# A four-layer decoder step on one core: cache transfers placed between weight tiles, and weight splits placed ahead of a triangular solution

## The chip, the cores and the metric

The kernel runs on one core of a Trainium2 chip. The metric is the device time of one execution in microseconds (us). The core has five engines with an instruction queue each: TensorE (PE, matrix products; its weight loads are listed as PEld), VectorE (DVE), ScalarE (ACT), GpSimd (POOL) and SyncE (SP). An engine works through its queue in order: an instruction that waits holds up all that stand behind it. Nearly all DMA transfers are issued from SP's queue (SPq in the rows) and carried out by 16 DMA engines.

## The reference

One step of a trunk of four layers, for a prompt of 256 tokens and 8 samples of 4 tokens, 288 columns in all, 1024 wide, in float32. Layer i mixes tokens by sliding-window attention (i mod 3 = 0: layers 0 and 3), a gated delta rule (layer 1) or a gated linear recurrence (layer 2). A feed-forward part stands before and behind each mixer.

```
for i in range(4):
    x = x + 0.5 * swiglu(rms(x), w_in[i, 0], w_out[i, 0])    # 1024 -> 2 x 2816 -> 1024
    x = x + mixer_i(rms(x))
    x = x + 0.5 * swiglu(rms(x), w_in[i, 1], w_out[i, 1])

# attention, sample group: the caches hold the last 128 keys and values
kk = concat([cache_k, k]);  vv = concat([cache_v, v])        # 128 + 4 rows
o  = softmax_with_sink(mask(q kk^T)) vv
new_cache_k, new_cache_v = kk[:, 4:], vv[:, 4:]              # outputs

# delta rule, prompt group, chunks of 64, 16 value heads
a   = strict_lower((k*beta) k^T) * decay
sol = triangular_solve(1 + a, [v*beta, k*beta*exp(gcum)])
```

So 124 of the 128 rows of every new cache are old rows, copied from the input to the output.

## The kernel before

**The weight stream.** Weights come from DRAM once and are the bulk of the traffic. The class Stream holds two lists: chunks (a raw tile of 128 x 4 x 256 float32, 512 KB, one DMA at L51) and jobs (half a chunk each in the feed-forward stages). Four raw tiles exist (RAW = 4). A job is split first: ACT writes the rounded part hi (L67), then DVE the rest lo = raw - hi (L68). PE then runs twelve matmuls into one accumulator: for each of four slices of 128 rows hi times the high part of the activations (L93), hi times their low part (L94), and lo times their high part (L95). Up to two jobs are split ahead of the one that PE works on (AHEAD = 2, three buffers each for hi and lo). When both jobs of a raw tile are split, the load of the next tile into its buffer is written down, and SP issues it once the buffer is free. The evacuations of the accumulators and all mixer work stand between the jobs.

**Order.** The code is recorded, and a scheduler then fixes each engine's order from what depends on what and from the place in the code. `tc.high_priority(n)` moves what is recorded in it to an earlier place, by n steps; PRIO is 5000. `tc.issue_after(ins)` keeps what is recorded in it behind the instruction `ins` on that instruction's engine. Within what these allow, an engine's order is fixed when the program is built.

**Attention caches** (layers 0 and 3). load_values loads all cached values into one tile vc (L402, 1 MB) and stores rows 4 to 127 of it to the output (L403). cache_unit, called four times with two samples each, does the same for the keys (kc, L407 and L408, 256 KB each) and transposes them. The scheduler moves these transfers forward as far as their buffers are free: SP issues several of them in the feed-forward stage ahead of the attention.

**Delta net** (layer 1, 800 to 1194 us). Its jobs come in the order gates, k, q, half of z, v, the other half of z. When the last k is there, DVE forms the triangular blocks and solve_unit inverts 32 x 32 diagonal blocks, 128 at a time: they go through DRAM into a layout with one block per partition (L953 to L956), DVE does 31 elimination steps of products (L965) and subtractions (L968) on the tile X, a copy transposes it (L969), and the result goes back through DRAM (L970 to L978). merge_unit then joins the 32-blocks to 64-blocks on PE (L989, L993). All of this is recorded at high priority, PRIO. sample_inverse_unit does the small inverse of the samples (matmuls L931, L933, L936 on tiles iv). Then the eight heads follow: conv on each v, v_unit (L1033 transposes the values), core_unit (the chunks of the prompt) and sample_unit with the samples' states (loaded at L1044). conv is L676 to L686.

Of the kernel before, what the change touches and what calls it, by code (L numbers as in the profile page):

```python
# [11 lines left out]
AF = mybir.ActivationFunctionType  # L12
ALU = mybir.AluOpType
# [2 lines left out]
T = 288  # L16
D = 1024
DFF = 2816
EPS = 1e-6
RAW, AHEAD, NT = 4, 2, 6  # L20
CW = 256
# [2 lines left out]
class Stream:  # L24

    def __init__(self, nc, raw, split, psum):
        self.nc, self.raw, self.split_pool, self.psum = nc, raw, split, psum
        self.chunks, self.jobs = [], []  # L30
        self.loaded, self.tiles, self.left = 0, {}, {}
        self.nsplit, self.parts = 0, {}
        self.njob = 0
        self.accs = {}
        self.pooled = set()
        self.held, self.mms, self.tags = [], [], {}

    def chunk(self, loads):
        self.chunks.append(loads)
# [6 lines left out]
    def load(self, upto):  # L46
        while self.loaded < min(upto, len(self.chunks)):
            c = self.loaded
            t = self.raw.tile([128, 4, CW], F32, tag="raw", name="raw", bufs=RAW)
            for sl, src in self.chunks[c]:  # L50
                self.nc.sync.dma_start(out=sl(t), in_=src)  # L51
            self.tiles[c] = t
            self.loaded += 1

    def split_to(self, upto):
        while self.nsplit < min(upto, len(self.jobs)):
            j = self.nsplit
            chunk, view, nk, m = *self.jobs[j][:3], self.jobs[j][8]
            self.load(chunk + 1)
            src = view(self.tiles[chunk])  # L60
            hi = self.split_pool.tile([128, 4, 128], F32R, tag="hi", name="hi", bufs=AHEAD + 1)
            lo = self.split_pool.tile([128, 4, 128], F32R, tag="lo", name="lo", bufs=AHEAD + 1)
            h, l = hi[:, :nk, :m], lo[:, :nk, :m]
            if len(src.shape) == 4:
                h = h.rearrange("p k (a b) -> p k a b", a=src.shape[2])
                l = l.rearrange("p k (a b) -> p k a b", a=src.shape[2])
            self.nc.scalar.activation(out=h, in_=src, func=AF.Copy)  # L67
            (self.nc.gpsimd if j in self.pooled else self.nc.vector).tensor_tensor(out=l, in0=src, in1=h, op=ALU.subtract)  # L68
            self.parts[j] = hi, lo
            self.nsplit += 1  # L70
            self.left[chunk] -= 1
            if not self.left[chunk]:
                self.tiles.pop(chunk)
                self.load(chunk + 1 + RAW)
# [28 lines left out]
PRIO = 5000  # L103
# [4 lines left out]
def trunk(ctx: ExitStack, tc: tile.TileContext, I, consts, O):  # L108
    nc = tc.nc
# [12 lines left out]
        def tile(shape, dt, tag, name):  # L122
            return psum.tile(shape, dt, tag=tag, name=name, bufs=PSUM_BUFS[tag])

    st = Stream(nc, raw, split, Acc)

    def misc(tag="ma"):
        return Acc.tile([128, 512], F32, tag, tag)
# [12 lines left out]
    class Slabs:  # L141


        def __init__(self, dt):
            self.dt, self.t = dt, {}
# [43 lines left out]
    def w_in_group(w, c0, key, evacs, m=128):  # L189

        for a in range(0, len(evacs), 2):
            n, c1, cs = len(evacs[a:a + 2]), c0 + a * m, []
            for kc in range(2):
                src = w[kc * 512:(kc + 1) * 512, c1:c1 + n * m].rearrange("(k p) c -> p k c", p=128)
                cs.append(st.chunk([((lambda t, n=n: t[:, :, :n * m]), src)]))
            if key not in begun:
                st.tags.update({(key, c1, e): "c%d" % e for e in range(n)} if TG else {})
            cells = [(kc, e) for kc in range(2) for e in range(n)]
            for kc, e in cells if key not in begun else sorted(cells, key=lambda c: c[1]):
                st.job(cs[kc], col(e, m), 4, xs_of(key, range(kc * 4, kc * 4 + 4)), (key, c1, e),  # L200
                       kc == 0, kc == 1, evacs[a + e], m=m)
            begun.add(key)
# [191 lines left out]
    def swa(i, j):  # L394
        key = ("m", i)
        w = I["swa_w_in"][j]
        L = {}

        def load_values():
            L["vc"] = mx(2048, "vc", 1).rearrange("p (b f) -> p b f", b=8)  # L400
            L["kT8"] = mx(2048, "kT8", 1).rearrange("p (g b j) -> p g b j", g=2, b=8)
            nc.sync.dma_start(out=L["vc"], in_=I["cache_swa_v"][j].rearrange("b j g d -> j b (g d)"))  # L402
            nc.sync.dma_start(out=O[8][j, :, 0:124].rearrange("b j g d -> j b (g d)"), in_=L["vc"][4:128])  # L403

        def cache_unit(b):
            kc = mx(512, "kc", 2).rearrange("p (b f) -> p b f", b=2)
            nc.sync.dma_start(out=kc, in_=I["cache_swa_k"][j, b:b + 2].rearrange("b j g d -> j b (g d)"))  # L407
            nc.sync.dma_start(out=O[7][j, b:b + 2, 0:124].rearrange("b j g d -> j b (g d)"), in_=kc[4:128])  # L408
            ps = misc()
            for a in range(2):  # L410
                for gp in range(2):
                    PE.transpose(ps[:, (gp * 2 + a) * 128:(gp * 2 + a + 1) * 128],
                                 kc[:, a, gp * 128:(gp + 1) * 128], ident)
            S.activation(out=L["kT8"][:, :, b:b + 2, :], in_=ps.rearrange("p (g b j) -> p g b j", g=2, b=2),
                         func=AF.Copy)
# [19 lines left out]
        def ev_kv(ps, m):  # L435
            if m == 0:
                L["kv"] = half()
                L["m4"] = mx(1024, "m4", 1)
                L["vtok"] = L["m4"][:, 0:512].rearrange("p (c f) -> p c f", c=2)
                L["ktok"] = L["m4"][:, 512:768]  # L440
                tables()
            if m < 2:
                rope(L["kv"][:, m], ps, "")
            else:
                V.tensor_tensor(out=L["kv"][:, m], in0=ps[:, :T], in1=nrm[key]["rbc"], op=ALU.mult)
            if m == 3:
                kv_tok_unit()
# [129 lines left out]
        def q_jobs(m0):  # L577
            for kc in range(2):
# [6 lines left out]
                for e in range(2):  # L585
                    st.job(c, (lambda t, e=e: t.rearrange("p k (a h d) -> p k a h d", a=2, h=2)[:, :, :, e]), 4,
                           xs_of(key, range(kc * 4, kc * 4 + 4)), (key, "q", m0 + e), kc == 0, kc == 1,
                           lambda ps, m=m0 + e: ev_q(ps, m))

        w_in_group(w, 1024, key, [lambda ps, m=m: ev_kv(ps, m) for m in range(4)])  # L590
        for m0 in (0, 2, 4):
            q_jobs(m0)
# [15 lines left out]
    def gdn(i, j):  # L608
        key = ("m", i)
        w = I["gdn_w_in"][j]  # L610
        L = {"st": {}, "vs": {}, "vt": {}, "u": {}}
# [628 lines left out]
        def run():  # L1240
            with tc.tile_pool(name="early", bufs=1, reuse_waits="tile") as M[1]:
                history()
                norm_run(key, False)
                st.run(34 + 8 * ZE - NJ)
                sample_inverse_unit()
            NW[0] = 7
            with tc.tile_pool(name="late", bufs=1, reuse_waits="tile") as M[1]:
                st.run(16)
                cores(0, 4)
                st.run(16)  # L1250
                cores(4, 8)
                st.run(32 - 8 * ZE)
                for kh in range(KS // 2):
                    gate(kh)
                st.run(2 * KS)
                for kh in range(KS // 2, 8):
                    gate(kh)
                st.run(32 - 2 * KS)
# [479 lines left out]
```

## Time and profile before

| | us |
|---|---|
| median of 3 runs | 2683.88 |
| lowest, highest | 2674.12, 2688.52 |
| the profiled execution: time | 2682.05 |
| the profiled execution: span | 2680.2 |
| PE busy in the span | 2575.3 (96%) |
| DVE busy in the span | 1763.5 (66%) |
| mean granted clock of PE | 0.976 of full speed |

The span runs from the first to the last instruction that the profiler saw; the profiled execution's time is 1.85 us more. PE's matmuls overlap, so a matmul's listed length (0.30 us) is longer than the distance at which the next one starts. The granted clock (PEclk) is 1.00 at 2.4 GHz and 0.50 at 1.2 GHz; it is 1.00 for most of the program. A high busy share of PE says that little can be won by moving work; what can be won shows in the short stretches in which PE waits, and in those at clock 0.50 that follow them.

### The profile page before, as it was taken

How to read it: one execution, taken by the hardware profiler on the slowest of the kernel's cores; microseconds unless marked ns; L12 is line 12 of the kernel's file. 1: busy time of each engine (PE TensorE's matmuls, PEld its weight loads, DVE VectorE, ACT ScalarE, POOL GpSimd, SP SyncE). 2: the span in 40 equal slices, each digit the busy share in tenths (PEclk: the TensorE clock that was granted, in tenths of full speed). 3: DMA queues.
4: the chain of work that ended last, by engine and by line, in shares of the span. 5: the costliest groups of instructions: out<-in, count | busy, mean ns of one | idle time of the engine just before them, and what ended most of it. 6: DMA issues, size and time to landing. Idle time of an engine off the chain costs nothing.

```text
span 2680.2 us, 52736 instructions
## 1 busy us (share of the span) xinstructions
PE 2575.3 (96%) x20268; PEld 2430.8 (91%) x20268; DVE 1763.5 (66%) x3772; ACT 1413.6 (53%) x3129; POOL 250.3 (9%) x404
## 2 busy tenths in 40 slices
PE   7999999999999799999999999888999999999998
PEld 6999799999997677689999999676899999979998
DVE  5666776666567756667666656877666665667655
ACT  4555555455455356665555544666455554465543
POOL 1000100000002134430000000443000000010000
PEclk9999999999999898899999999999999999999999
DMA  6555345555553354455555555344555555533553
GB/s 191 166 160 168 82 133 166 165 163 168 162 161 105 93 145 123 123 155 164 162 165 163 168 166 162 98 129 130 178 160 165 165 166 165 172 94 111 171 163 124
DMA packets 442370, 400.14 MB, mean 149 GB/s; under 512 B 24491, under 2 KB 439973, under 8 KB 442117
## 3 DMA queue, kind: packets, MB, share of 16 engines
q1 hardware_dynamic: 441492, 395.66, 49.0%
q8 instruction: 159, 2.61, 0.4%
q10 hardware_dynamic: 624, 1.11, 0.1%
q14 instruction: 95, 0.77, 0.1%
HBM read 374.64 MB, written 22.07 MB: 148 GB/s over the span
## 4 chain that ended last, share of the span: by engine, by line
PE 76%; issue 11%; DVE 6%; DMA 2%; POOL 2%; ACT 2%; SPq 0%; DVEq 0%; POOLq 0%; ACTq 0%
PE acc L93 22%; PE acc L95 22%; PE acc L94 22%; DVE lo L68 1%; DMA raw<-in_ffn_w_in_dram 1%; DMA kc<-in_cache_swa_k_dram 1%; PE c L513 1%; PE c L1163 1%; PE s L528 1%; PE c L1454 0%; PE ma L520 0%; DVE acc L682 0%; ACT hi L67 0%; PE c L1168 0%; DVE W L1380 0%
## 5 line engine op out<-in xcount | busy, mean ns | idle before, releaser
L93 PE MATMUL acc<-sl,hi 128*128 128x288 f32 x5384 | 1617.1, 301 | 21.6 <-ACT hi L67 13.4
L95 PE MATMUL acc<-sl,lo 128*128 128x288 f32 x5384 | 1607.8, 299 | 19.1 <-DVE lo L68 18.9
L94 PE MATMUL acc<-sl,hi 128*128 128x288 f32 x5384 | 1612.2, 299 | 1.8 <-DVE sl L1487 1.8
L67 ACT ACTIVATE hi<-raw 128x512 fp32r<-128x512 f32 (+1 forms) x1378 | 853.2, 621 | 992.6 <-PE acc L94 920.8
L68 DVE TENSOR_TENSOR lo<-raw,hi 128x512 fp32r<-128x512 f32 (+1 forms) x1378 | 952.6, 693 | 592.6 <-ACT hi L67 537.3
L95 PEld LDWEIGHTS acc<-sl,lo 128*128 128x128 f32 x5384 | 1025.9, 191 | 32.9 <-DVE lo L68 21.9
L93 PEld LDWEIGHTS acc<-sl,hi 128*128 128x128 f32 x5384 | 1021.8, 190 | 34.7 <-ACT hi L67 16.1
L94 PEld LDWEIGHTS acc<-sl,hi 128*128 128x128 f32 x5384 | 1023.4, 190 | 14.0 <-issue 10.1
L272 POOL TENSOR_TENSOR r<-v,roots 128x3 f32<-128x3 f32 x5 | 5.8, 1162 | 1867.3 <-DVE v L292 1867.3
L362 DVE TENSOR_TENSOR sil<-acc,sil 128x288 f32<-128x288 f32 x176 | 79.8, 457 | 54.3 <-PE acc L95 50.9
L355 DVE TENSOR_TENSOR sil<-acc,rbc 128x288 f32<-128x288 f32 x176 | 79.7, 457 | 50.5 <-PE acc L95 50.2
L364 DVE TENSOR_TENSOR sl<-sil,sl 128x288 fp32r<-128x288 f32 x176 | 78.9, 452 | 0.0
L356 ACT ACTIVATE sil<-sil 128x288 f32<-128x288 f32 x176 | 77.6, 445 | 2.0 <-DVE sil L355 1.9
L363 ACT ACTIVATE sl<-sil 128x288 fp32r<-128x288 f32 x176 | 77.5, 444 | 0.6 <-DVE sil L362 0.6
L242 ACT ACTIVATE sl<-x,gT 128x288 fp32r<-128x288 f32 x96 | 51.0, 536 | 26.0 <-DVE x L379 15.4
L682 DVE SCALAR_TENSOR_TENSOR acc<-buf,cw,acc 128x312 f32<-128x312 f32 x96 | 57.8, 606 | 4.2 <-ACT acc L680 2.0
L245 DVE SCALAR_TENSOR_TENSOR sl<-x,gT,sl 128x288 fp32r<-128x288 f32 x96 | 50.6, 532 | 0.2
L498 ACT ACTIVATE e<-e,m 128x128 f32<-128x128 f32 (+1 forms) x72 | 32.6, 454 | 17.0 <-DVE m L495 16.8
L258 ACT ACTIVATE sq<-x 128x288 f32<-128x288 f32 x91 | 38.7, 431 | 5.1 <-DVE x L379 5.1
L255 DVE TENSOR_TENSOR ssq<-ssq,sq 128x288 f32<-128x288 f32 x84 | 37.9, 451 | 0.1
L1113 POOL TENSOR_TENSOR st<-st,ex 128x512 f32<-128x512 f32 x32 | 35.7, 1136 | 17.4 <-PE ma L1080 17.4
L495 DVE CUSTOM_DVE_ANT_0 e<-c,sl,sink 128x128 f32<-128x128 f32 (+1 forms) x72 | 27.8, 419 | 13.4 <-PE c L513 10.6
(435 smaller groups left out, 1847.8 us busy)
## 6 DMA issues: line engine op xcount, KB each, us to landing
raw<-in_ffn_w_in_dram SPq DMA_DIRECT2D x352, 512.0 KB
raw<-in_ffn_w_out_dram SPq DMA_DIRECT2D x128, 512.0 KB
raw<-in_ffn_w_out_dram SPq DMA_DIRECT2D x64, 384.0 KB
raw<-in_gdn_w_in_dram SPq DMA_DIRECT2D x48, 512.0 KB
raw<-in_hgrn_w_in_dram SPq DMA_DIRECT2D x32, 512.0 KB
out_dram<-st SPq DMA_DIRECT2D x24, 512.0 KB
raw<-in_swa_w_in_dram SPq DMA_DIRECT2D x32, 256.0 KB
raw<-in_swa_w_out_dram SPq DMA_DIRECT2D x32, 256.0 KB
```

What stands on the lines that cost most here:

```text
L67: self.nc.scalar.activation(out=h, in_=src, func=AF.Copy)
L68: (self.nc.gpsimd if j in self.pooled else self.nc.vector).tensor_tensor(out=l, in0=src, in1=h, op=ALU.subtract)
L93: mm(ps, hi[:, i, :m], xh(), start=start and i == 0, stop=False)
L94: mm(ps, hi[:, i, :m], xl(), start=False, stop=False)
L95: self.mms.append(mm(ps, lo[:, i, :m], xh(), start=False, stop=stop and i == last).ins)
L242: S.activation(out=h[m], in_=x[:, m], func=AF.Identity, scale=g)
L355: V.tensor_tensor(out=t, in0=ps[:, :T], in1=nrm[key]["rbc"], op=ALU.mult)
L356: S.activation(out=t, in_=t, func=AF.Silu)
L362: V.tensor_tensor(out=t, in0=ps[:, :T], in1=t, op=ALU.mult)
L363: S.activation(out=h, in_=t, func=AF.Copy)
L364: V.tensor_tensor(out=l, in0=t, in1=h, op=ALU.subtract)
L682: V.scalar_tensor_tensor(out=a[:, 0:312], in0=b[:, t:t + 312], scalar=cw[:, 32 * t + mt:32 * t + mt + 1], in1=a[:, 0:312], op0=ALU.mult, o ...
```

## The change

Two things, independent of each other.

1. **Cache transfers of the attention layers.** Stream notes the DMA of each raw tile (loads). load_values and cache_unit wrap their DMAs in issue_after, so that each stands on SP behind a given raw tile of the feed-forward stage ahead of the attention: the load of vc behind tile 16, its store behind tile 24, the key loads behind tiles 28, 36, 44 and 52, and their stores six tiles later. L["before"] counts where that stage begins (FFN_CHUNKS is its number of tiles: 22 x 2 for w_in and 24 for w_out). Each store of 124 rows becomes two, of 112 and of 12 rows.
2. **Splits in the delta net's first part.** While the jobs up to the second z group are recorded, with the sample inverse, Stream.first is 2 * PRIO: the splits (L67, L68 before; L71, L72 now) are recorded at that priority, ahead of the solution at PRIO. Elsewhere first is 0.

```diff
@@ Stream @@
+        self.loads = {}
+        self.first = 0
...
-                self.nc.sync.dma_start(out=sl(t), in_=src)
+                self.loads[c] = self.nc.sync.dma_start(out=sl(t), in_=src).ins
...
-            self.nc.scalar.activation(out=h, in_=src, func=AF.Copy)
-            (self.nc.gpsimd if j in self.pooled else self.nc.vector).tensor_tensor(out=l, in0=src, in1=h, op=ALU.subtract)
+            with self.tc.high_priority(self.first):
+                self.nc.scalar.activation(out=h, in_=src, func=AF.Copy)
+                (self.nc.gpsimd if j in self.pooled else self.nc.vector).tensor_tensor(out=l, in0=src, in1=h, op=ALU.subtract)
@@ swa @@
+        def behind(n):
+            return tc.issue_after(st.loads[L["before"] + n])
+
+        def store(dst, src):
+            for a, n in ((0, 112), (112, 12)):
+                nc.sync.dma_start(out=dst[:, a:a + n].rearrange("b j g d -> j b (g d)"), in_=src[4 + a:4 + a + n])
...
-            nc.sync.dma_start(out=L["vc"], in_=I["cache_swa_v"][j].rearrange("b j g d -> j b (g d)"))
-            nc.sync.dma_start(out=O[8][j, :, 0:124].rearrange("b j g d -> j b (g d)"), in_=L["vc"][4:128])
+            with behind(16):
+                nc.sync.dma_start(out=L["vc"], in_=I["cache_swa_v"][j].rearrange("b j g d -> j b (g d)"))
+            with behind(24):
+                store(O[8][j], L["vc"])
...
-            nc.sync.dma_start(out=kc, in_=I["cache_swa_k"][j, b:b + 2].rearrange("b j g d -> j b (g d)"))
-            nc.sync.dma_start(out=O[7][j, b:b + 2, 0:124].rearrange("b j g d -> j b (g d)"), in_=kc[4:128])
+            with behind(28 + 4 * b):
+                nc.sync.dma_start(out=kc, in_=I["cache_swa_k"][j, b:b + 2].rearrange("b j g d -> j b (g d)"))
+            with behind(34 + 4 * b):
+                store(O[7][j, b:b + 2], kc)
...
+        L["before"] = len(st.chunks) - FFN_CHUNKS
@@ gdn, run @@
+                st.first = 2 * PRIO
                 st.run(34 + 8 * ZE - NJ)
                 sample_inverse_unit()
+                st.first = 0
```

The orders of the engines stand as follows. SP's queue in the first feed-forward stage, before, from the load of the cached values on (x3 means three in a row):

```order
L402 DMA vc<-in_cache_swa_v_dram 128x8x256
L51 DMA raw<-in_ffn_w_in_dram 128x4x256 x3
L403 DMA out_dram<-vc 124x8x256
L407 DMA kc<-in_cache_swa_k_dram 128x2x256
L51 DMA raw<-in_ffn_w_in_dram 128x4x256
L407 DMA kc<-in_cache_swa_k_dram 128x2x256
L408 DMA out_dram<-kc 124x2x256
```

The same place now, with twelve further raw tiles ahead of the first cache transfer:

```order
L54 DMA raw<-in_ffn_w_in_dram 128x4x256 x12
L416 DMA vc<-in_cache_swa_v_dram 128x8x256
L54 DMA raw<-in_ffn_w_in_dram 128x4x256 x8
L410 DMA out_dram<-vc 112x8x256
L54 DMA raw<-in_ffn_w_in_dram 128x4x256
L410 DMA out_dram<-vc 12x8x256
L54 DMA raw<-in_ffn_w_in_dram 128x4x256 x3
L423 DMA kc<-in_cache_swa_k_dram 128x2x256
L54 DMA raw<-in_ffn_w_in_dram 128x4x256 x6
L410 DMA out_dram<-kc 112x2x256
```

The cache transfers have moved from the stage's start to places between its raw tiles, at least one tile apart.

DVE's queue in the middle of the solution, before, around the elimination step with blocks of 12 and 13 columns:

```order
L968 TENSOR_TENSOR X<-X,tmp 128x10x12 x2
L965 TENSOR_TENSOR tmp<-A,X 128x130
L965 TENSOR_TENSOR tmp<-A,X 128x117
L968 TENSOR_TENSOR X<-X,tmp 128x10x13
L968 TENSOR_TENSOR X<-X,tmp 128x9x13
```

The same steps now:

```order
L983 TENSOR_TENSOR tmp<-A,X 128x120
L72 TENSOR_TENSOR lo<-raw,hi 128x512
L983 TENSOR_TENSOR tmp<-A,X 128x120
L986 TENSOR_TENSOR X<-X,tmp 128x10x12 x2
L983 TENSOR_TENSOR tmp<-A,X 128x130
L983 TENSOR_TENSOR tmp<-A,X 128x117
L72 TENSOR_TENSOR lo<-raw,hi 128x512
L986 TENSOR_TENSOR X<-X,tmp 128x10x13
L986 TENSOR_TENSOR X<-X,tmp 128x9x13
```

Lo parts of the weight stream (L72) now stand between the products and subtractions of the solution.

PE's queue at the end of the merge and the sample inverse, before (L993 is the merge, L1149 the first head):

```order
L95 MATMUL acc<-sl,lo 128x288
L931 MATMUL s<-iv 32x32 x16
L993 MATMUL c_10992<-sl,tmp 32x32
L933 MATMUL s<-iv 32x32 x16
L936 MATMUL s<-iv,cst 128x512
L993 MATMUL c_10992<-sl,tmp 32x32 x31
L1149 MATMUL c_12291<-cst,sl 64x128 x8
```

The sample inverse's last two products now (L951 and L954, which were L933 and L936):

```order
L99 MATMUL acc<-sl,lo 128x288
L951 MATMUL s<-iv 32x32 x16
L97 MATMUL acc<-sl,hi 128x288
L98 MATMUL acc<-sl,hi 128x288
L99 MATMUL acc<-sl,lo 128x288
L97 MATMUL acc<-sl,hi 128x288
L98 MATMUL acc<-sl,hi 128x288
L99 MATMUL acc<-sl,lo 128x288
L954 MATMUL s<-iv,cst 128x512
```

The sample inverse, which stood inside the merge, now stands ahead of it among stream matmuls. The merge's first matmul (L989 before, L1007 now) has 5725 stream matmuls ahead of it before and 5865 now, counted from the program's start; between the merge's last matmul and the first transposes of values (L1033, now L1051) stood 139 and stand 33.

## Rows read from the trace of the kernel before

**Rows 1.** The page: its span, and each engine's busy us, share and instructions.

```profile
span 2680.2 us, 52736 instructions
...
PE 2575.3 (96%) x20268; PEld 2430.8 (91%) x20268; DVE 1763.5 (66%) x3772; ACT 1413.6 (53%) x3129; POOL 250.3 (9%) x404
```

**Rows 2.** Stretches: us, busy PE, PEld, DVE, ACT, POOL; PEclk, DMA share, GB/s.

```profile
20.00:24.00 4.00, 4.00 (x31) 3.89 (x30) 3.93 (x9) 1.49 (x4) 1.64 (x2) 1.00 1.00 333
32.00:38.00 6.00, 5.60 (x42) 5.36 (x42) 4.62 (x10) 4.72 (x10) 0.00 (x0) 1.00 0.26 87
49.20:52.40 3.20, 3.20 (x12) 2.82 (x12) 0.94 (x2) 0.18 (x1) 0.00 (x0) 0.50 0.52 156
...
100.00:110.00 10.00, 10.00 (x77) 10.00 (x76) 6.52 (x12) 5.04 (x10) 0.00 (x0) 1.00 0.48 152
```

**Rows 3.** Waits, 40 to 60 us: who waited for whom, us, times, longest.

```profile
ACT hi L67 <- DMA raw<-in_ffn_w_in_dram: 14.1, 2, 8.4
...
PE acc L93 <- ACT hi L67: 8.4, 2, 5.2
```

**Rows 4.** Timeline of SP's queue, 5 to 110 us: start, us, instruction.

```profile
16.77 0.42 SPq L402 DMA_DIRECT2D vc<-in_cache_swa_v_dram  x1
21.08 6.65 SPq L51 DMA_DIRECT2D raw<-in_ffn_w_in_dram  x3
27.82 0.41 SPq L403 DMA_DIRECT2D out_dram<-vc  x1
```

**Rows 5.** Timeline of SP and ACT, 121.5 to 131 us.

```profile
121.66 8.37 SPq L51 DMA_DIRECT2D raw<-in_ffn_w_in_dram  x4
...
129.87 0.63 ACT L67 ACTIVATE hi<-raw 128x512 fp32r<-128x512 f32 x1 [0.96 <-PE acc L94]
```

**Rows 6.** Stretches of the feed-forward stage ahead of the last layer.

```profile
1890.00:1896.00 6.00, 6.00 (x47) 6.00 (x46) 5.41 (x13) 4.97 (x10) 0.00 (x0) 1.00 0.27 94
1916.90:1919.90 3.00, 2.94 (x12) 2.94 (x13) 2.86 (x9) 0.69 (x2) 0.00 (x0) 0.50 0.05 18
```

**Rows 7.** Waits of PE, 1895 to 1925 us.

```profile
PE acc L93 <- ACT hi L67: 5.0, 2, 2.7
```

**Rows 8.** Stretches in the delta net.

```profile
887.30:903.20 15.90, 0.02 (x2) 0.02 (x1) 15.86 (x84) 0.00 (x0) 0.00 (x0) 0.50 0.00 1
903.20:906.30 3.10, 3.10 (x13) 3.10 (x14) 3.10 (x18) 0.50 (x1) 0.00 (x0) 0.51 0.08 5
800.00:940.00 140.00, 117.03 (x1231) 99.01 (x1230) 102.40 (x337) 63.22 (x154) 27.53 (x79) 0.91 0.36 100
```

**Rows 9.** Timeline of PE; in brackets the idle time before and its releaser.

```profile
903.18 0.61 PE L95 MATMUL acc<-sl,lo 128*128 128x288 f32 x1 [15.88 <-DVE lo L68]
```

**Rows 10.** DVE by line, 882 to 915.3 us: busy us, mean ns, idle before.

```profile
L682 DVE SCALAR_TENSOR_TENSOR acc<-buf,cw,acc 128x312 f32<-128x312 f32 x10 | 5.4, 537 | 0.0
L68 DVE TENSOR_TENSOR lo<-raw,hi 128x512 fp32r<-128x512 f32 x7 | 4.8, 680 | 0.0
```

**Rows 11.** Line L965: ns min/median/max, first and last start, forms.

```profile
L965 DVE TENSOR_TENSOR tmp<-A,X x60: 163/242/281, 882.3 to 913.2; 128x110 f32<-128x110 f32 x5, 128x120 f32<-128x120 f32 x5, 128x126 f32<-128x126 f32 x5, 128x56 f32<-128x56 f32 x4
```

**Rows 12.** Timeline of SP's queue, 820 to 1000 us.

```profile
914.54 0.41 SPq L970 DMA_DIRECT2D XD<-X  x1
...
919.94 1.00 SPq L974 DMA_DIRECT2D xc<-XD  x2
...
947.45 4.09 SPq L1044 DMA_DIRECT2D st<-in_state_gdn_dram  x4
```

**Rows 13.** Lines L989 and L1033 on PE: ns min/median/max, first and last start.

```profile
L989 PE MATMUL c<-xc,sl x128: 190/191/213, 926.2 to 934.1; 32*32 32x32 f32 x128
...
L1033 PE MATMUL ma<-cst,v x32: 270/272/331, 971.4 to 1145.0; 128*128 128x128 f32 x32
```

**Rows 14.** PE by line, 926 to 971 us: busy us, mean ns, idle before.

```profile
L936 PE MATMUL s<-iv,cst 32*128 32x512 f32 x2 | 1.9, 1062 | 0.7 <-ACT iv L934 0.7
...
L933 PE MATMUL s<-iv 32*32 32x32 f32 x32 | 1.2, 192 | 0.8 <-DVE iv L932 0.8
```

More of the change, by code (lines that the diff above doesn't have):

```diff
@@ L18 @@
 DFF = 2816
+FFN_CHUNKS = DFF // 128 * 2 + 24
 EPS = 1e-6
@@ L24, with __init__ @@
 class Stream:
-    def __init__(self, nc, raw, split, psum):
-        self.nc, self.raw, self.split_pool, self.psum = nc, raw, split, psum
+    def __init__(self, tc, raw, split, psum):
+        self.tc, self.nc, self.raw, self.split_pool, self.psum = tc, tc.nc, raw, split, psum
         self.chunks, self.jobs = [], []
@@ L123, in tile @@
             return psum.tile(shape, dt, tag=tag, name=name, bufs=PSUM_BUFS[tag])
-    st = Stream(nc, raw, split, Acc)
+    st = Stream(tc, raw, split, Acc)
     def misc(tag="ma"):
```

## The prediction

> **What bounds the kernel now.** I read the page first: TensorE (PE) is busy for 96% of the span [rows 1], so only time in which PE stands still, or runs at the lower of its two clock levels, can be won back. In the steady feed-forward stretch 77 matmuls start in 10 us, one per 0.13 us, at full clock [rows 2]: nothing there can get faster by reordering. So I looked, with the table of stretches and the waits of PE, for the stretches in which PE waits. All its idle time is 105 us (span less busy), but the order of the instructions changes in three places only: SP's queue in the feed-forward stages ahead of the two attention layers, the engines' orders in the delta net (800 to 1194 us), and nothing else. Three waits lie there.
>
> The first is at 44 to 56 us. PE waits 8.4 us for ACT's hi parts, and ACT waits for weights [rows 3]. What keeps the weights: the load of vc is issued at 16.8 us, ahead of three weight tiles, and its store at 27.8 us [rows 4]. From 32 to 38 us the DMA engines are busy for 0.26 of their time and move 87 GB/s, against 1.00 and 333 GB/s at 20 to 24 us [rows 2]: about 4 of the 16 engines work, on a transfer of 124 rows, and the weights wait behind it. The second is the same picture before the last layer: 0.27 and 94 GB/s [rows 6], and 5.0 us of PE waiting [rows 7].
>
> The third is in the delta net. From 887.3 us PE does nothing for 15.9 us, and what ends it is a lo part of VectorE (DVE) [rows 8, 9]. DVE is busy for 15.86 us of this wait [rows 8]: it works on the triangles' solution, which in the order of before stands ahead of the splits.
>
> **The change, part by part.** *Cache transfers.* They are the same bytes, moved behind weight tiles 16, 24, 28 and so on of the stage, and ten more DMA issues for the 12-row rests. SP has the time: it mostly waits for buffers. What hides a transfer is the slack of a weight tile: one issued at 121.7 us is first split at 129.9 us, 8.2 us later [rows 5], while 512 KB at 333 GB/s [rows 2] takes 1.6 us. With two tiles in a burst and some start-up I read 3 to 4 us. The 1 MB of vc adds 3.1 us at that rate, which leaves 1 us or more. If the cover fails, each of the four large transfers costs 1 to 2 us.
>
> A store of 112 rows is in no row of the trace. Its price lies between that of the 124-row store, 0.9 MB at 87 GB/s = 10.5 us, and that of a 128-row load, 0.9 MB at 333 GB/s = 2.8 us. I take the second: 112 is seven times 16, and the 128-row transfers, eight times 16, fill all engines. The 12-row rest of 96 KB costs 1.1 us even at 87 GB/s. The Trainium skill (DMA: Bandwidth & Descriptors, "Why a DMA increments its semaphore by 16 and not by 1") gives the number of engines as the largest one up to 16 that divides the slowest dimension: 4 for 124, 16 for 112, 12 for 12. The share of 0.26 agrees for 124; for 112 and 12 no run here shows it. By the page the sum stays as below; were the row of the 124-row store the better guide, the third rival's time would hold.
>
> So both waits go. First: 8.4 us, and after each of its two parts PE ran at half clock: two stretches of 3.2 us at 0.50 (the one from 49.2 us in [rows 2], the other from 56.4 us), in which about half the time is lost, 3.0 us. Second: 5.0 us of waiting, and 3 us at 0.50 [rows 6], 1.5 us. Together 11.4 + 6.5 = **17.9 us**. Nothing is late next: behind these waits PE has its steady matmuls. The compared orders show no other engine's row moved before 800 us.
>
> *Splits ahead of the solution.* This removes at most the 15.9 us, plus 1.5 us for the 3.1 us at 0.51 that follow [rows 8]: 17.4 us. But the splits now delay the solution, and somebody waits for that. I count between the first triangle operation (882.3 us [rows 11]) and the copy that ends the solution. Before, there are 7 splits; in the changed order, 19. Twelve more at 0.68 us [rows 10] are 8.2 us. Two more conv steps at 0.54 us [rows 10], one iv product, three z products and some copies add 4.5 us. DVE had hardly a gap there, so the solution ends about 12.7 us later than its 915 us (the store of its result is issued at 914.5 us and leaves after the copy [rows 12]): at 928 us. From there the results go through DRAM: the reload of xc is issued at 919.9 us [rows 12] and PE's first merge matmul (L989) runs at 926.2 us [rows 13]. That is 11 us after the copy, but PE was not waiting, so the trip may be as short as 8. The merge is ready at 936 to 939 us.
>
> When does PE come to the merge? It saves 17.4 us, but has 140 more stream matmuls ahead of it (5865 instead of 5725 since the program's start), 18.6 us, and the sample inverse, 4 us (L933 and L936 are busy for 1.2 and 1.9 us with waits of 0.8 and 0.7 us [rows 14], L931 as L933; in part they overlap the stream). So 926.2 - 17.4 + 18.6 + 4 = 931.4 us, and it waits 4.5 to 7.5 us there; I take 6. Such a wait lowers the clock, 1.5 us as after the others. And DVE's new order mixes splits, which need buffers that PE frees, with work that PE waits for; between 800 and 940 us DVE is busy for 102 of 140 us [rows 8], so I put 3.5 us on further waits of DVE inside the solution. What is left is 17.4 - 6 - 1.5 - 3.5 = **6.4 us**. The bounds: 0 us if DVE's own waits take another 6.4 us, 12 us with none and the short trip.
>
> Behind the merge the work is the same: the first head's values (L1033, 971.4 us [rows 13]) stood 139 stream matmuls behind the merge, now 33; these matmuls are what has gone ahead. The first sample states (L1044) are issued at 947.5 us after the merge [rows 12], and now have less time until their use. Their first 1 MB takes 3.1 us at 333 GB/s plus start-up, against about 14 us until the first head's values: covered, otherwise 0 to 3 us. The eight heads that follow are a chain through PE, DVE and ACT with short waits throughout; I take it to start earlier and be as long as before.
>
> The sum against the profiled execution: 2682.05 us (span 2680.2 us [rows 1]) - 17.9 - 6.4 = 2657.8 us. The median of the three runs, 2683.88 us, lies 1.8 us above the profiled one, so I forecast 2659.5, say 2659 us.
>
> **Rivals.** *The wait moves in full.* For it: DVE is the engine that PE waited for, and it gets 12.7 us more work in the same place. Against it: PE brings 22.6 us of work along. If DVE needs 6 to 20 us more than I allow, the delta net gains nothing or loses up to 13 us, and only the cache part remains: 2664 to 2678, most likely 2668 us.
>
> *The solution costs nothing.* If DVE's extra work fits in gaps I took for filled, all 17.4 us go: 2648 us. Against it: hardly a gap is left there [rows 8].
>
> *The change does not do what it says to the transfers.* If 112 rows ran on few engines, or the store still held up tiles, half of the 17.9 us would stay: 2668 us. For it: no row shows such a store. Against it: the 128-row transfers, which fill all engines [rows 2].
>
> *Slower than before.* A split on DVE waits for ACT's hi part, which waits for a buffer that PE frees. If each of the 12 splits new in the solution held DVE for a whole round (a PE job of twelve matmuls, 1.6 us, plus 0.6 on ACT and 0.7 on DVE, so 2.2 us more than its own 0.7), the solution would end 26 us later again. The delta net would lose about 20 us, the total would be 2684; only with each split held for over 3.4 us more, 41 us in all, does it reach 2698 us, slower by 0.5%. Against it: two splits are kept ahead.
>
> **How the numbers follow.** Chances: my forecast, with gains of 1 to 12 us in the delta net, 0.55; the wait moves in full 0.22; the transfers stay half as costly 0.10; all gained 0.08; slower 0.05. The range reaches from all gained (2648, less 2 for the scatter of the runs) to the upper end of the moved wait: 2646 to 2678 us. Against 2683.88 us, 0.5%, about what a measurement of this kernel can tell from no change, is 13.4 us: faster means below 2670.5. Forecast, all gained, half of the moved wait and most of the transfers' rival lie there: 0.76. Same: 0.19. Slower: 0.05.
>
> **What the changed profile would show.** Right: no wait of PE for ACT's hi at 40 to 60 us or around 1900 us; a DMA share far above 0.26 while vc is stored; no 15.9 us wait for lo; instead some 4 to 10 us of PE waiting around 925 to 940 us, at the inverse or at the merge's first matmul (L1007 there); the first L1051, as L1033 is called there, some 24 us earlier than 971 us, of which 11 come from the first stage. Wrong: new waits of PE for hi after a cache load or store; a wait at the merge of 15 us or more; or the heads' chain growing longer, as waits of PE in 960 to 1180 us. That last is the step I know least of: the orders there are permuted, too.

## The result and the profile after

The changed kernel takes 2641.82 us in the median of four executions (2632.71, 2640.79, 2642.85 and 7416.7 us) against 2683.3 us before: a ratio of 0.9845 with a 95% interval of 0.9823 to 0.9867. That is 41.5 us less, and below the low end of the prediction's range (2646 us). The execution of 7416.7 us is a slow one whose cause is not known; without it the median is 2640.79 us, 42.5 us less than before. A later measurement of the same kernel beside others gave 2639.93 us against 2683.36 us, 0.9836 (0.9816 to 0.9857).

The page of the profiled execution (2632.71 us), its span and its engines:

```profile
span 2630.9 us, 52770 instructions
...
PE 2549.8 (97%) x20268; PEld 2411.8 (92%) x20268; DVE 1763.5 (67%) x3772; ACT 1414.1 (54%) x3129; POOL 246.4 (9%) x404
```

PE is busy for 25.5 us less than in [rows 1], with the same 20268 matmuls. That alone says that part of the gain is clock and not waiting; the mean granted clock rose from 0.976 to 0.989.

To find where the time went I compared the starts of the n-th stream matmul in the two traces. Four stretches carry 47 of the 49.3 us between the two spans:

| stretch | before, us | after, us | change | predicted |
|---|---|---|---|---|
| first feed-forward stage, to stream matmul 240 | 62.6 | 50.2 | -12.4 | -11.4 |
| around 1900 us, stream matmuls 10800 to 11200 | 63.0 | 54.1 | -8.9 | -6.5 |
| delta net, front: from stream matmul 5200 to the first transposes of values | 184.7 | 176.7 | -8.0 | -6.4 |
| delta net, heads: from the first to the last transposes of values | 173.6 | 155.9 | -17.7 | 0 |

**The cache part.** The stretches that answer to [rows 2, 6], and the first vc store at its new place (86 to 92 us), in the trace of after (columns as in [rows 2]):

```profile
32.00:38.00 6.00, 6.00 (x45) 5.78 (x45) 4.62 (x11) 4.73 (x10) 0.00 (x0) 1.00 0.38 108
86.00:92.00 6.00, 6.00 (x47) 6.00 (x47) 3.29 (x6) 2.89 (x7) 0.00 (x0) 1.00 1.01 334
1849.00:1855.00 6.00, 6.00 (x48) 6.00 (x47) 4.96 (x10) 3.99 (x8) 0.00 (x0) 1.00 0.57 165
```

While the 112 rows leave (the store is issued at 84.1 us), all DMA engines are busy (1.01, 334 GB/s), and PE works through it at full clock. The last layer's transfers are gone from 1850 us; they now stand at 2115 us and later. The Trainium skill (DMA: Bandwidth & Descriptors, "Why a DMA increments its semaphore by 16 and not by 1") gives 16 engines for 112 rows, and this row agrees. No wait of PE is left at 40 to 60 us, in place of the 8.4 us in [rows 3]; ACT now waits for PE there, and no longer for weights:

```profile
ACT hi L71 <- PE acc L98: 10.0, 13, 1.0
DVE lo L72 <- ACT hi L71: 4.9, 7, 1.0
```

**The front of the delta net.** The timeline of PE, the row that answers to [rows 9] (in brackets the idle time and its releaser), and the start of the copy that ends the solution:

```profile
912.08 1.12 PE L875 MATMUL c<-sl 128*64 128x64 f32 x16 [7.83 <-DVE sl L880]
```

```profile
L987 DVE COPY tmp<-X x1: 1086/1086/1086, 919.5 to 919.5; 128x1024 f32<-128x1024 f32 x1
L1007 PE MATMUL c<-xc,sl x128: 191/191/212, 928.0 to 935.6; 32*32 32x32 f32 x128
```

The wait of 15.9 us is gone, and one of 7.83 us stands in its place: PE waits for a bank that DVE's product of the chunks (L880) frees, and that product stands behind steps of the solution in DVE's queue. The merge (L1007) follows the copy by 8.5 us, and PE does not wait for it.

**The heads.** Here is what the prediction did not see. One row for each kernel, over the heads:

```profile
971.40:1145.00 173.60, 161.74 (x1205) 121.20 (x1206) 116.56 (x274) 106.97 (x371) 79.71 (x132) 0.91 0.44 123
```

```profile
949.50:1105.40 155.90, 147.93 (x1201) 109.43 (x1201) 113.87 (x274) 107.82 (x379) 81.10 (x134) 1.00 0.53 146
```

Before (first fence), the clock is 0.91 in the mean, so some 2 x 0.09 x 173.6 = 31 us of the heads ran at half clock; after, none. That costs 0.09 x 173.6 = 15.6 us, and PE's idle time fell from 11.9 us (173.6 - 161.7) to 8.0 us. Together that is 19.5 us, enough for the 17.7 us. PE's waits in the heads, before and after:

```profile
PE c L1168 <- ACT co L1165: 4.6, 3, 3.5
PE s L1193 <- ACT co L1054: 3.0, 1, 3.0
PE ma L1098 <- ACT t L1091: 1.5, 1, 1.5
```

```profile
PE c L1186 <- ACT co L1183: 4.0, 8, 1.3
PE ma L1140 <- POOL km L1135: 1.3, 3, 0.6
PE ma L1116 <- DVE rh L1104: 1.1, 1, 1.1
```

The longest wait of before is 3.5 us, that of after 1.3 us. Where the two long ones come from, the timeline of before shows around the second:

```profile
1082.02 1.28 POOL L1117 TENSOR_TENSOR km<-kr,cst 128x512 fp32r<-128x512 f32 x1
...
1083.25 1.45 POOL L272 TENSOR_TENSOR bf<-bv,roots 128x4 f32<-128x4 f32 x1
1084.74 0.69 ACT L1054 ACTIVATE co<-co,bf 128x128 f32<-128x128 f32 x2 [4.37 <-POOL bf L272]
...
1085.19 0.47 PE L1193 MATMUL s<-cst,co 128*128 128x128 f32 x1 [3.00 <-ACT co L1054]
```

POOL computes the roots bf of a head's norm (the factors that scale its columns) behind its updates of the samples' states (L1113) and a product (L1117); ACT waits 4.37 us for bf, and PE 3.00 us for ACT. The wait of 3.5 us is the same picture at 1002 to 1006 us, with 4.80 us of ACT.

### The profile page after: what moved, and what is told of

It is laid out like the page before. It is cut to its first block, busy times and chain, and to the rows that moved or that the text cites. A ratio compares the mean times of both kernels' runs of the same rounds, so it can differ in the third digit from the quotient of the medians.

```text
span 2630.9 us, 52770 instructions
## 1 busy us (share of the span) xinstructions
PE 2549.8 (97%) x20268; PEld 2411.8 (92%) x20268; DVE 1763.5 (67%) x3772; ACT 1414.1 (54%) x3129; POOL 246.4 (9%) x404
## 4 chain that ended last, share of the span: by engine, by line
PE 78%; issue 11%; DVE 6%; POOL 2%; ACT 2%; DMA 1%; DVEq 0%; POOLq 0%; ACTq 0%; SPq 0%
PE acc L97 23%; PE acc L99 23%; PE acc L98 23%; DVE lo L72 1%; PE s L545 1%; PE c L530 1%; PE c L1186 0%; DVE W L1400 0%; PE ma L537 0%; PE c L1190 0%; DVE F L1366 0%; PE c L1192 0%; PE c L1181 0%; PE c L1474 0%; ACT hi L71 0%
## 5 line engine op out<-in xcount | busy, mean ns | idle before, releaser
L71 ACT ACTIVATE hi<-raw 128x512 fp32r<-128x512 f32 (+1 forms) x1378 | 854.3, 621 | 963.0 <-PE acc L98 934.4
L72 DVE TENSOR_TENSOR lo<-raw,hi 128x512 fp32r<-128x512 f32 (+1 forms) x1378 | 948.4, 689 | 571.2 <-ACT hi L71 515.1
L359 DVE TENSOR_TENSOR sil<-acc,rbc 128x288 f32<-128x288 f32 x176 | 79.6, 456 | 50.1 <-PE acc L99 49.8
L700 DVE SCALAR_TENSOR_TENSOR acc<-buf,cw,acc 128x312 f32<-128x312 f32 x96 | 59.0, 625 | 11.9 <-ACT acc L698 11.5
```

The costliest lines, as they stand in the source:

```text
L359: V.tensor_tensor(out=t, in0=ps[:, :T], in1=nrm[key]["rbc"], op=ALU.mult)
L700: V.scalar_tensor_tensor(out=a[:, 0:312], in0=b[:, t:t + 312], scalar=cw[:, 32 * t + mt:32 * t + mt + 1], in1=a[:, 0:312], op0=ALU.mult, o ...
```

## The experiments

Three questions: what each part of the change is worth, which half of the cache part does it, and what made the heads shorter. The heads are measured in all runs as above.

### The cache part alone

```diff
-                st.first = 2 * PRIO
                 st.run(34 + 8 * ZE - NJ)
                 sample_inverse_unit()
-                st.first = 0
```

> The changed kernel without its second part (first stays 0). The engines' orders outside SP's queue are those of before. My theory: both feed-forward waits go, which the trace of the changed kernel puts at 12.3 us in the first stage and 8.7 us in the second, so about 2662 us; the delta net stays as before, with the 15.9 us wait for a lo part and some 41 us at half clock between the first and the last transposes of values (L1033 before), which stay 173.6 us apart. Rival: part of the shorter heads comes from the cache part (other timing of the DMA queue); then that distance falls below 165 us here too and the time below 2655 us.

Measured: 2650.54 us against 2678.7 us, 0.9895 (0.9878 to 0.9912), 28 us. The wait for the lo part is still there (15.9 us) and the front as long as before (184.4 us), but the heads take 164.1 us. So the rival was nearer, and one statement in the expectation was wrong: the complete listings show that the cache part also changes the engines' orders in the heads (of PE, DVE, ACT and POOL), where the scheduler decides them anew. The 41 us at half clock in the expectation count 10 us that lie ahead of the first transposes; between the transposes it is 31 us. PE's waits in these heads, and the heads' row:

```profile
PE c L1186 <- ACT co L1183: 4.5, 2, 3.5
PE ma L1116 <- ACT t L1109: 2.1, 1, 2.1
```

```profile
956.30:1120.40 164.10, 153.43 (x1221) 113.85 (x1222) 116.59 (x278) 108.93 (x382) 79.63 (x132) 0.96 0.47 130
```

Of the two long waits one is left. Half clock falls from 31 to 2 x 0.04 x 164.1 = 13 us, idle time from 11.9 to 10.7 us: (31 - 13) / 2 + 1.2 = 10 us, and 9.5 us were measured. The Trainium skill (TensorE: Matmul & The Clock Gate, "Terms") describes a lowered clock as one that passes K of every N pulses, 4/8 being half rate; the clock of 0.50 in [rows 2, 8] agrees.

### The splits alone

The cache lines are put back as they were (L402, L403, L407 and L408 of before).

> The changed kernel without its first part: cache transfers stand where they stood before, whole stores of 124 rows. My theory: the delta net alone gains what the two traces show, 25.5 us, so about 2658 us: the 15.9 us wait is gone, a wait of some 8 us of PE for a product of VectorE behind the solution's steps stands at its place, and the transposes of values span 156 us with at most 5 us at half clock among them. Rival: the shorter heads are a chance of that one execution; then the span stays near 174 us and the time comes to about 2675 us.

Measured: 2659.27 us, 0.9928 (0.9907 to 0.9948), 19.4 us. The heads span 156.0 us at clock 1.00, the front 176.8 us with the 7.8 us wait. The mechanism is as expected, and the orders of PE, DVE, ACT and POOL in front and heads are those of the changed kernel. The two parts do not add up: 28.2 + 19.4 = 47.6 us against 43.4 us for both in the later measurement, since each alone shortens the heads.

### Place or size of the stores

Whole stores at the new places:

```diff
-            for a, n in ((0, 112), (112, 12)):
+            for a, n in ((0, 124),):
```

> The changed kernel with cache stores of 124 rows at the new places (not 112 and 12). My theory: a store of 124 rows runs on few DMA engines (0.9 MB at 87 GB/s, 10.5 us) and holds up the weight tiles behind it wherever it stands, so PE waits for hi parts come back behind the vc store, 3 to 8 us in each of the two stages, 2648 to 2658 us. Rival: the distance between the transfers does the work; then it stays within 3 us of the changed kernel, 2639 to 2645 us.

Measured: 2654.46 us, 0.9906 (0.9889 to 0.9923), some 15 us more than the changed kernel's 2639.93 (19 us by the two ratios). A wait is back behind each of the two vc stores, at 96 us and at 2169 us:

```profile
PE acc L97 <- ACT hi L71: 5.6, 1, 5.6
```

```profile
PE acc L97 <- ACT hi L71: 5.5, 1, 5.5
```

And the DMA engines during the first of them:

```profile
88.00:90.00 2.00, 2.00 (x18) 2.00 (x17) 1.15 (x2) 1.16 (x3) 0.00 (x0) 1.00 0.27 96
```

While the 124 rows leave, the DMA share is 0.27, as at the old place in [rows 2, 6]. With the half clock behind the waits the two places lose 8.3 and 7.8 us against the changed kernel. So the place alone moves the waits and keeps most of them: of 12.4 + 8.9 us it leaves some 5 us of gain. Against the splits alone, measured beside it, whole stores at the new places gain 4.8 us.

Split stores at the old places (the keys' store likewise):

```diff
-            nc.sync.dma_start(out=O[8][j, :, 0:124].rearrange("b j g d -> j b (g d)"), in_=L["vc"][4:128])
+            for a, n in ((0, 112), (112, 12)):
+                nc.sync.dma_start(out=O[8][j, :, a:a + n].rearrange("b j g d -> j b (g d)"), in_=L["vc"][4 + a:4 + a + n])
```

> The kernel before with each cache store in 112 and 12 rows, at the old places. My theory: the stores then leave in about 3 us instead of 10.5, the weights no longer stand behind them, and most of both waits goes: a gain of 5 to 9 us in the first stage and of 5 to 9 us in the second, 2662 to 2669 us. Rival: the place matters (vc and kc ahead of the weights, whatever their stores take, and SP's queue held by a store that waits for its load): the waits stay at more than half, 2670 to 2679 us.

Measured: 2663.31 us, 0.9938 (0.9923 to 0.9954), 17.3 us. The stretch of [rows 2] that had a share of 0.26:

```profile
32.00:38.00 6.00, 6.00 (x45) 5.77 (x44) 5.00 (x11) 4.99 (x10) 0.00 (x0) 1.00 0.82 272
```

PE has no wait left at 20 to 62 us. The first stage is 11.9 us shorter and the second 8.9 us, as in the changed kernel (12.4 and 8.9). So the rival is out: cutting the stores in two does what the cache part does for these stages, and the places add half a microsecond. The orders of PE, DVE, ACT and POOL are those of before throughout, and so are the heads: 173.5 us at clock 0.91.

### Does the arrival or the order set the heads?

The first part of the change for the last layer alone, without the splits:

```diff
-            return tc.issue_after(st.loads[L["before"] + n])
+            return tc.issue_after(st.loads[L["before"] + n]) if j else ExitStack()
...
-            for a, n in ((0, 112), (112, 12)):
+            for a, n in ((0, 112), (112, 12)) if j else ((0, 124),):
```

> The first part of the change in the last layer alone; the first layer's cache transfers stand as before, and the splits too. The run with the cache part alone had the heads' transposes 164.1 us apart with 13.7 us at half clock, against 173.6 and 30.7 in the kernel before, at the same orders of PE, VectorE, ScalarE and GpSimd. If the earlier arrival in the delta net made that (the first stage ends 12 us sooner), it is gone here: 173 us, 30 us at half clock, and 8.9 us gained in the last layer alone, about 2670 us. Rival: an execution scatters that much by itself; then the heads may lie anywhere between 156 and 174 us and the time between 2655 and 2672 us.

Measured: 2665.63 us, 0.9943 (0.9926 to 0.9959); heads of 164.1 us at clock 0.96, although the front begins 11 us later than with the cache part alone (783.0 us instead of 771.8). Neither the earlier arrival nor scatter: the heads are those of the run with the cache part alone to a tenth of a microsecond, and its orders of PE, DVE, ACT and POOL are the same ones. Three orders occur in more than one run (some of the runs come below), each with its own length, whatever the arrival:

| orders of PE, DVE, ACT, POOL in the heads | runs | heads, us |
|---|---|---|
| those of before | before; split stores at old places | 173.6, 173.5 |
| cache part without splits | cache part alone; last layer alone; splits at PRIO | 164.1, 164.1, 165.2 |
| changed kernel | changed kernel twice; splits alone; whole stores; later products at 12000 | 155.9, 155.9, 156.0, 156.0, 157.4 |

Between orders the heads differ by 7 us or more, within one order by at most 1.5 us. The 157.4 us are the last case of "What the hardware showed".

### POOL's work ahead of the roots

The update of the samples' states on 8 of each 128 columns, on the kernel before:

```diff
-                G.tensor_tensor(out=sta[:, b:b + 2], in0=sta[:, b:b + 2],
-                                in1=L["egs"][:, b:b + 2, 2 * kh:2 * kh + 2].unsqueeze(3).to_broadcast([128, 2, 2, 128]), op=ALU.mult)
+                G.tensor_tensor(out=sta[:, b:b + 2, :, 0:8], in0=sta[:, b:b + 2, :, 0:8],
+                                in1=L["egs"][:, b:b + 2, 2 * kh:2 * kh + 2].unsqueeze(3).to_broadcast([128, 2, 2, 8]), op=ALU.mult)
```

> The kernel before, with GpSimd's update of the samples' states (L1113) on 8 of each 128 columns: this leaves out most of the states' decay. The orders of PE, VectorE and SP are those of before. My theory: in the heads ScalarE waits for the roots bf that GpSimd computes behind these updates, PE waits for ScalarE (3.5 us at 1002 us, 3.0 us at 1082 us), and after each such wait the clock is at half for 10 to 14 us; with short updates these waits fall below 1.5 us, the half-clock time among the heads falls from 41 us to under 12 us, and the transposes of values span 152 to 160 us instead of 173.6: 2664 to 2672 us. Rival: the order of PE's own queue in the heads makes the waits; it is the same here, so the time stays within 4 us of before.

The same edit on the changed kernel, as a control:

> The changed kernel with the update of the samples' states on 8 of each 128 columns, as in the run on the kernel before (most of the states' decay is left out); orders of PE, VectorE, ScalarE and SP as in the changed kernel. My theory: the 17 us that short updates took off the heads of the kernel before were its two waits of 3.5 and 3.0 us and the half clock behind them; the changed kernel has no such waits, so the same cut gives nothing here: heads of 152 to 157 us, 2637 to 2645 us. Rival: GpSimd's time is in the heads' chain as such; then they get shorter by 10 us or more, below 146 us.

And the opposite, each update twice on the changed kernel:

```diff
-                G.tensor_tensor(out=sta[:, b:b + 2], in0=sta[:, b:b + 2],
+                for _ in range(2):
+                    G.tensor_tensor(out=sta[:, b:b + 2], in0=sta[:, b:b + 2],
...
```

> The changed kernel with each update of the samples' states done twice (the states are decayed twice), some 4.6 us more of GpSimd work in each head, and PE, VectorE, ScalarE and SP in the order of the changed kernel. My theory: ScalarE waits for the roots behind these updates again, PE for ScalarE, waits of 3 us or more come back in several heads and with them half clock of 7 to 14 us each: heads of 175 us or more, 2660 us or more. Rival: the waits in the heads come from the orders of PE and VectorE; then the heads stay within 5 us of 156.

| | time, us | ratio to before | heads, us | clock in the heads |
|---|---|---|---|---|
| before | 2678.7 | 1 | 173.6 | 0.91 |
| before, short updates | 2663.88 | 0.9941 (0.9922 to 0.9961) | 156.8 | 0.98 |
| changed | 2639.93 | 0.9836 (0.9816 to 0.9857) | 155.9 | 1.00 |
| changed, short updates | 2637.78 | 0.9827 (0.9803 to 0.9851) | 154.3 | 1.00 |
| changed, double updates | 2675.33 | 0.9973 (0.9959 to 0.9988) | 188.8 | 0.88 |

In all three, PE, DVE and SP keep the order of their base; POOL's differs around the updates, and ACT's in one place in the first. The same cut takes 16.8 us off the heads of before and 1.6 us off those of the changed kernel: what it removed were the waits behind POOL and their half clock, not POOL's work as such. In the kernel before with short updates, the heads' row and PE's waits with the largest totals:

```profile
970.30:1127.10 156.80, 151.56 (x1205) 112.74 (x1205) 109.90 (x274) 106.52 (x371) 54.23 (x132) 0.98 0.49 136
```

```profile
PE ma L1098 <- ACT t L1091: 2.1, 1, 2.1
PE c L1168 <- ACT co L1165: 1.3, 3, 0.6
```

Doubling the updates brings it all back. The heads' row, PE's waits and one chain of them, in the kernel with double updates:

```profile
952.50:1141.30 188.80, 166.00 (x1201) 124.10 (x1201) 119.36 (x274) 108.42 (x379) 110.54 (x162) 0.88 0.44 122
```

```profile
PE ma L1141 <- POOL km L1136: 10.6, 6, 2.9
PE c L1187 <- ACT co L1184: 9.7, 5, 5.0
```

```profile
985.93 5.21 POOL L1132 TENSOR_TENSOR st<-st,ex 128x512 f32<-128x512 f32 x4
991.10 1.00 POOL L276 TENSOR_TENSOR bf<-bv,roots 128x4 f32<-128x4 f32 x1
...
992.14 0.40 ACT L1072 ACTIVATE co<-co,bf 128x128 f32<-128x128 f32 x1 [5.65 <-POOL bf L276]
...
992.85 0.69 PE L1187 MATMUL c<-u,sl 64*64 64x128 f32 x4 [5.00 <-ACT co L1184]
```

Updates for 5.21 us, then the roots, ACT 5.65 us late, PE 5.00 us late. PE idles for 22.8 us of these heads instead of 8.0, and about 2 x 0.12 x 188.8 = 45 us run at half clock. The first term is 14.8 us, the second 22.7 us, together 37.5 us; the heads grew by 32.9 us. Part of the idle time (2.8 us) lies in half clock and is counted twice; the rest of the difference stays open.

### What bounds the front

The later products of the chunks ahead of the solution too:

```diff
-        QG = 6500
+        QG = 12000
```

> The changed kernel with the later q products of the chunks (QG) at priority 12000 instead of 6500, ahead of the solution as the splits are. My theory: VectorE is the limit in this stretch. The 7.8 us wait of PE for such a product goes, but the solution ends 2 to 5 us later, PE comes to the merge 8 us earlier and waits there, in all within 5 us of the changed kernel: 2637 to 2647 us. Rival: PE was held by the order alone; then the 7.8 us and the 5 us that the half clock costs behind it are gained, 2628 to 2632 us.

Measured: 2640.85 us, 0.9852 (0.9834 to 0.9869), within the first bound, but it tells nothing on the theory: ahead of the heads only one split moved, by one step of the solution at 887 us, well ahead of the wait, and the 7.8 us stand as they were. Why the scheduler leaves the product there stays open.

Eight lo parts on POOL (first is the number of the delta net's first job):

```diff
+        st.pooled.update(range(first + 24, first + 40, 2))
         group(6048, ev_gates, 0, 1)
```

> The changed kernel with eight lo parts of the stretch of the solution on GpSimd instead of VectorE, which frees VectorE of 8 x 0.69 = 5.5 us. My theory: VectorE's work ahead of the end of the solution is what PE waits for; the 7.8 us wait falls to 2 to 4 us, the half clock behind it goes in part, 2633 to 2638 us. Rival: GpSimd's lo parts (its 128x512 products take 1.04 us) come late and PE waits for them instead: 2642 us or more.

Measured: 2646.83 us, 0.9876 (0.9855 to 0.9897), 6 us more than the run just above, which was measured beside it. The wait falls to 4.2 us, but the edit does not do what was meant: six of the eight parts stand ahead of the first operation of the solution (877.2 us), so DVE still does 16 splits inside it instead of 19, and the solution ends 150.3 us after the front's start, not 146.7 us. So the run does not show whether DVE's work is the limit. The time is in the rival's range, but PE waits for no lo part of POOL; the parts take 1.27 to 1.45 us each, not 1.04. Of the waits at the merge, the one of 1.3 us for L1013 stands in the changed kernel too; the one of 1.5 us for L1009 is new, and that of 1.4 us was 0.4 us:

```profile
PE c L875 <- DVE sl L880: 4.2, 1, 4.2
PE c L1007 <- ACT tmp L1009: 1.5, 1, 1.5
PE c L1167 <- ACT tmp L1009: 1.4, 1, 1.4
PE c L1011 <- ACT sl L1013: 1.3, 1, 1.3
```

The splits at the priority of the solution only (5000 is PRIO):

```diff
-                st.first = 2 * PRIO
+                st.first = 5000
```

> The changed kernel with the splits at the priority of the solution (PRIO) instead of twice that. Splits then pass the later part of the solution only. My theory: the stretch up to the heads lies between the two kernels (177 us in the changed one, 185 before), with a shorter wait for the q products and some wait for lo parts in its place; the heads get a third order, and their length is 156 to 174 us by whether a wait of 3 us or more stands in it: 2640 to 2660 us. Rival: half of the priority does all of the front's gain, since fewer splits lie inside the solution: below 2637 us.

Measured: 2662.46 us, 0.9912 (0.9885 to 0.9939). Neither theory: PE waits for a lo part as long as before, so the front gains nothing (188.8 us), and the heads take 165.2 us. No third order came up: the heads' orders are those of the cache part alone, with its wait of 3.5 us.

```profile
902.40 0.61 PE L99 MATMUL acc<-sl,lo 128*128 128x288 f32 x1 [16.92 <-DVE lo L72]
```

### The changed kernel again

> The changed kernel once more, beside the others of this call. If the heads' length follows from the orders alone, the transposes of values span 156 us with no half clock among them, as in the two other runs with these orders: 2639 to 2645 us. Rival: they scatter from execution to execution, 156 to 174 us.

Measured: 2639.93 us, as told above; the heads are again 155.9 us at clock 1.00. Its front is 181.8 us instead of 176.7 us, so the 8.0 us of the first profile are not the rule: with this execution the front gains 2.9 us, and the four terms sum to 12.5 + 8.9 + 2.9 + 17.7 = 42 us (its first stage ends at 50.1 us), the 41.5 us of the medians. Over all runs, the front took 184.7 to 187.4 us in the three executions with the orders of before, and 176.7 to 182.4 us in the six with the orders of the changed kernel; the means are 185.9 and 180.1 us, about 6 us apart.

None of the runs beats the changed kernel beyond its interval without leaving work out.

## Why the prediction was wrong

**What bounds the kernel: half right.** The three waits that it named were real and went. It listed waits and priced the half clock only behind those three. The heads of before run at 0.91 of full clock, and none of its rows has the clock of that stretch, where the trace of before shows (columns as in [rows 2]):

```profile
1000.00:1050.00 50.00, 46.19 (x338) 35.29 (x341) 33.08 (x76) 31.55 (x109) 22.22 (x37) 0.90 0.49 138
1050.00:1100.00 50.00, 44.55 (x301) 33.61 (x293) 29.97 (x67) 28.11 (x94) 23.48 (x40) 0.83 0.36 101
```

**Cache part: right, a little small.** Predicted 17.9 us; 12.4 + 8.9 = 21.3 us measured, and 17.3 us in the timing of split stores alone. The choice between the two bounds for the 112-row store (2.8 or 10.5 us) was right: share 1.01 at 334 GB/s. Its rival, that the transfers stay half as costly, is out. The first stage's 12.4 us are the upper end: in three other executions with the transfers as before it ended at 60.3 to 60.8 us, not 62.6, so the gain is 10 to 12 us. In the second stage the sum left out two short waits: all of PE's idle time there is 6.1 us, not 5.0, and with 1.7 us for the 3.4 us at half clock that makes 7.8 of the 8.9 us. The prediction credited place and row count together; the row count does the work.

**Splits ahead of the solution: right in size, wrong in place.** Predicted 6.4 us; the front gained 8.0 and 2.9 us in two executions, and about 6 us between the means over all runs. The trip from copy to merge was taken as 8 us or more and is 8.5 us. From the stretch's start, the solution's end moved by 19 us (127.5 to 146.7 us), not by the 12.7 us of work and the 3.5 us of waits; PE had also more to do by then and met the wait earlier, at the product L880 for 7.83 us, not at the merge for 6.

**The step that failed: "a chain through PE, DVE and ACT with short waits throughout; I take it to start earlier and be as long as before".** It is a chain with two long waits, 3.5 and 3.0 us, behind POOL, which the sentence does not even name, and with 31 us at half clock. The diff moves nothing in the heads by its words, but the scheduler ordered them anew with each of its two parts. The prediction ended on exactly that ("the orders there are permuted, too") and gave it neither a price nor a rival. The trace of before had both: the two waits and the half clock, 3.5 + 3.0 + 15.6 = 22 us, are about what a better order could give, and the runs show 17.7 us of it. With that term the sum of 24.3 us is 42 us.

**The rivals.** The moved wait took 7.83 us and its half clock; the solution needed 3 us more than was allowed for, less than the rival's 6 us. The solution costing nothing, the costly transfers and the slower case did not occur. The 0.76 for faster does not follow from its list: 0.55 + 0.08 + 0.11 and more than half of 0.10 make at least 0.79.

That the new order of the heads has no long wait is luck, a by-product. Nothing in the change aims at it, and the runs do not show why the scheduler found it.

## What to carry to other kernels

List not only the waits but the granted clock by stretch over the whole program, and price every stretch that a scheduler orders anew, even where the diff does not touch it: a wait of 3 us cost 8 to 10 us here. If a small instruction on a side engine (here the roots on POOL, 1.0 to 1.45 us) stands behind bulk work on that engine and ahead of a chain that ends at TensorE, it can set the chain's length, by 17 us here. Cut a store of 124 rows into 112 and 12 before moving it about: the cut alone gave 17.3 us here, the move alone some 5 us.

## What the hardware showed that was not expected

Behind the same wait the clock falls in one execution and not in another. At 797 to 801 us of the changed kernel PE waits 2.53 us in both of its profiled executions:

```profile
799.42 0.37 PE L97 MATMUL acc<-sl,hi 128*128 128x288 f32 x1 [2.53 <-DVE gt L807]
```

```profile
800.76 0.37 PE L97 MATMUL acc<-sl,hi 128*128 128x288 f32 x1 [2.53 <-DVE gt L807]
```

In the first the clock stays at 1.00 behind it, in the second it is 0.81 in the mean over the next 27 us:

```profile
799.40:826.00 26.60, 24.51 (x219) 20.04 (x220) 17.55 (x44) 17.00 (x39) 9.42 (x24) 1.00 0.29 82
```

```profile
800.80:828.20 27.40, 25.90 (x198) 20.64 (x198) 14.89 (x36) 15.85 (x37) 7.61 (x19) 0.81 0.27 79
```

So a stretch of one profile can be 5 us off from the next one of the same program. The heads repeat better, but not always to 0.1 us: with the orders of the changed kernel, and the same waits of at most 1.3 us, they ran at clock 1.00 in four executions, and in the fifth (later products at 12000) with 3.4 us at half clock:

```profile
949.10:1106.50 157.40, 149.48 (x1202) 110.73 (x1203) 114.31 (x274) 107.73 (x379) 80.98 (x134) 0.99 0.52 145
```
